# Token-major residual stream and output projections in a three-layer hybrid kernel

## The chip, the cores and the metric

One core of a Trainium2 chip. The metric is the device time of one launch, in microseconds (us), as the median of the runs shown. TensorE (PE in the profile), VectorE (DVE), ScalarE (ACT) and GpSimd (POOL) compute; SP issues most of the loads.

## What is computed

A sequence of 512 tokens of width 2048 passes through three layers, in float32. The first mixes attention (16 heads) with a gated recurrence (8 heads), the other two mix retention (6 heads), differential attention (4 heads) and a linear recurrence with a convolution. All have the same frame, and the first has a gated addition behind it:

```python
u = rmsnorm(h, g_pre);  z = u @ w_in          # z is split into q, k, v, gates, ...
y = concat(mixers(z)) @ w_out
h = h + rmsnorm(y, g_post)
# first layer only
gate = sigmoid(h @ w_pg);  e = p_l @ w_pp
h = h + rmsnorm(gate * e, g_ple)
```

The norms are over the 2048 channels of a token.

## The kernel before

Every large product is made of three: each float32 operand is split into a rounded part and a rest (`whi`, `wlo` for weights, `uh`, `ul` for activations), and `uh*whi + ul*whi + uh*wlo` is summed in PSUM. `wpiece` (line 212) loads a piece of weights of 512 KB on SP and splits it, ACT making `whi` (line 238) and DVE `wlo` (line 239). There are two raw buffers; while `self.extra` is set (the output stages of the first layer and of layer 0 of the second block) every third piece uses a set of its own.

TensorE's order is written by hand; the other engines are ordered by a scheduler by priority. Two products exist. `proj` (line 243) keeps weights as the stationary operand and gives channels by tokens, 128 x 512, in 16 steps over the input channels. `projT` (line 303) keeps activations stationary and gives tokens by channels; it is used for values, 256 columns at a time (`hg_round` line 580, `att_round` line 449, `qkv` line 1187), and for the last output projection.

The mixers run in the shadow of projections: they are generators in a queue (`add`, `unit`, `tick`, lines 111 to 129). Each projection step credits its time with `tick`, and when the credit exceeds `self.spacing` (2.9, 3.25 or 4.6 us by stage) one unit of mixing is emitted between matmuls. `gates` (line 731) forces units until the head that it needs is done.

Up to the last layer the residual stream `X` is channel-major (16 tiles of 128 channels by 512 tokens), as is `U`, its split. An output stage is `rows` (line 778): one `proj` of four tiles, five of two, then `proj_halves` (line 278) for the last two tiles, in two token halves. ACT squares every tile, POOL sums the squares (line 793), and `col_rstd` (line 766) sums them over channels with a matmul of ones (line 772) and takes Ln and Exp. `carry` (line 837) then has POOL scale each tile by the row factor (line 821), DVE add it to the stream (line 822), and ACT and DVE split the sum (`split`, lines 830 to 835), first for tokens 0 to 255, then for the rest. The next projection starts with twelve of its 16 steps on the first token half (`half_first`, `NH = 12`) and does their second half at its end. `spill` (line 859) stores the stream and squares it for the next norm; `stream_stats` (line 872) finishes that norm at step 12 of the recurrence's second projection (`lru`, line 1069).

The last output stage is `last_rows` (line 1388) and already token-major: `projT` for 1792 columns, the stream turned back by 64 transposes (line 1408), then the last 256 columns by token group (lines 1433 to 1435), where each group of 128 tokens ends with its sum, its factor (a power on POOL, line 1441) and its residual adds (line 1446).

The input stage is `load_x` (line 334): x comes token-major, TensorE turns it by 64 transposes (line 362), ACT and DVE split it, and it is stored channel-major for later.

## Time and profile before

| | us |
|---|---|
| median of 3 runs | 3137.11 (3136.86 to 3137.35) |
| the profiled execution | 3136.49 |
| its span, first to last instruction | 3134.7 |
| TensorE busy | 3053.4 (97%) |
| DVE / ACT / POOL busy | 1907.1 / 1521.9 / 808.4 |
| mean granted TensorE clock | 0.991 |

A profiled execution is a run of its own, so its time stands beside its span. Matmuls are pipelined: their durations overlap, and the distance between two starts is what one costs. Idle time of an engine matters only where the engine sets the end.

### The profile page before, as it was taken

How to read it: one execution, taken by the hardware profiler on the slowest of the kernel's cores; microseconds unless marked ns; L12 is line 12 of the kernel's file. 1: busy time of each engine (PE TensorE's matmuls, PEld its weight loads, DVE VectorE, ACT ScalarE, POOL GpSimd, SP SyncE). 2: the span in 40 equal slices, each digit the busy share in tenths (PEclk: the TensorE clock that was granted, in tenths of full speed). 3: DMA queues.
4: the chain of work that ended last, by engine and by line, in shares of the span. 5: the costliest groups of instructions: out<-in, count | busy, mean ns of one | idle time of the engine just before them, and what ended most of it. 6: DMA issues, size and time to landing. Idle time of an engine off the chain costs nothing. (4 is left out here: it accounts for less than half of the span.)

```text
span 3134.7 us, 45170 instructions
## 1 busy us (share of the span) xinstructions
PE 3053.4 (97%) x17004; PEld 2660.5 (85%) x17004; DVE 1907.1 (61%) x3321; ACT 1521.9 (49%) x2731; POOL 808.4 (26%) x838
## 2 busy tenths in 40 slices
PE   8999999999999999998899999999989999999998
PEld 7888888888888888887688888878877888888898
DVE  5778788577776327458775456542478654565434
ACT  5354343455556335446555434653465545346532
POOL 1555456110110204127430011011264200111101
PEclk9999999999999999999999999999999999999999
DMA  6222222332332533335342233243353322332433
GB/s 209 77 72 74 75 75 72 104 96 85 85 90 75 170 99 118 123 104 163 95 118 85 84 108 95 81 149 108 108 177 90 108 88 81 108 95 81 131 112 115
DMA packets 296776, 327.67 MB, mean 105 GB/s; under 512 B 17823, under 2 KB 277998, under 8 KB 296430
## 3 DMA queue, kind: packets, MB, share of 16 engines
q1 hardware_dynamic: 277518, 275.74, 28.4%
q0 software_dynamic: 16864, 45.37, 5.0%
q10 hardware_dynamic: 2176, 3.68, 0.4%
q8 instruction: 133, 2.18, 0.3%
q14 instruction: 85, 0.70, 0.1%
HBM read 292.23 MB, written 16.78 MB: 99 GB/s over the span
## 5 line engine op out<-in xcount | busy, mean ns | idle before, releaser
L239 DVE TENSOR_TENSOR wlo<-raw,whi 128x512 fp32r<-128x512 f32 x1028 | 806.5, 792 | 790.5 <-ACT whi L238 772.4
L270 PE MATMUL acc<-ul,whi 128*128 128x512 f32 (+1 forms) x3056 | 1167.6, 382 | 27.9 <-DVE ul L835 21.6
L269 PE MATMUL acc<-uh,whi 128*128 128x512 f32 (+1 forms) x3056 | 1183.3, 387 | 9.2 <-ACT whi L238 7.5
L271 PE MATMUL acc<-uh,wlo 128*128 128x512 f32 (+1 forms) x3056 | 1168.3, 382 | 14.1 <-DVE wlo L239 13.8
L238 ACT ACTIVATE whi<-raw 128x512 fp32r<-128x512 f32 x1028 | 635.8, 627 | 985.0 <-PE acc L270 570.1
L270 PEld LDWEIGHTS acc<-ul,whi 128*128 128x128 f32 x3056 | 580.5, 190 | 133.7 <-DVE ul L835 23.3
L271 PEld LDWEIGHTS acc<-uh,wlo 128*128 128x128 f32 x3056 | 579.2, 190 | 132.4 <-DVE wlo L239 20.7
L269 PEld LDWEIGHTS acc<-uh,whi 128*128 128x128 f32 x3056 | 580.0, 190 | 114.4 <-ACT whi L238 9.2
L318 PE MATMUL acct<-whi,uh 128*128 128x256 f32 (+1 forms) x1536 | 446.2, 290 | 1.7 <-DVE gt L738 1.1
L319 PE MATMUL acct<-wlo,uh 128*128 128x256 f32 (+1 forms) x1536 | 442.1, 288 | 1.6 <-DVE wlo L239 1.6
L320 PE MATMUL acct<-whi,ul 128*128 128x256 f32 (+1 forms) x1536 | 442.1, 288 | 0.0
L318 PEld LDWEIGHTS acct<-whi,uh 128*128 128x128 f32 x1536 | 294.8, 192 | 5.9 <-DVE gt L738 1.5
L319 PEld LDWEIGHTS acct<-wlo,uh 128*128 128x128 f32 x1536 | 294.9, 192 | 5.5 <-DVE wlo L239 1.8
L320 PEld LDWEIGHTS acct<-whi,ul 128*128 128x128 f32 x1536 | 294.7, 192 | 2.6
L742 POOL TENSOR_TENSOR mx<-mx,gt 128x512 f32<-128x512 f32 x48 | 65.3, 1362 | 599.1 <-ACT gt L739 591.9
L793 POOL TENSOR_TENSOR ssq<-ssq,sq 128x512 f32<-128x512 f32 x39 | 52.4, 1343 | 383.4 <-ACT sq L976 254.4
L821 POOL TENSOR_TENSOR mx<-mx,rbo 128x256 f32<-128x256 f32 x96 | 90.9, 984 | 80.5 <-ACT rbo L209 80.5
L635 POOL TENSOR_TENSOR w<-w,t 128x512 f32<-128x512 f32 x56 | 69.4, 1239 | 70.1 <-DVE zz L627 69.9
L1168 POOL TENSOR_TENSOR q<-q,rt 128x512 f32<-128x512 f32 x20 | 31.6, 1581 | 214.5 <-DVE rt L1167 208.9
L636 POOL TENSOR_TENSOR w<-w,t 128x512 f32<-128x512 f32 x56 | 78.5, 1402 | 19.6 <-DVE zz L628 19.6
L462 POOL TENSOR_TENSOR zsw<-zsw,ropes 80x512 f32<-80x512 f32 x16 | 28.1, 1757 | 214.0 <-DMA zsw<-q 115.8
L1168 POOL TENSOR_TENSOR k<-k,rt 128x512 f32<-128x512 f32 x20 | 31.6, 1579 | 140.9 <-DVE rt L1167 100.9
(388 smaller groups left out, 3906.9 us busy)
## 6 DMA issues: line engine op xcount, KB each, us to landing
raw<-in_w_in SPq DMA_DIRECT2D x304, 512.0 KB
raw<-in_w_out SPq DMA_DIRECT2D x88, 512.0 KB
raw<-in_w_in SPq DMA_DIRECT2D x120, 256.0 KB
raw<-in_w_pg SPq DMA_DIRECT2D x28, 512.0 KB
raw<-in_w_out SPq DMA_DIRECT2D x32, 256.0 KB
x<-x_stream POOLq DMA_DIRECT2D x32, 256.0 KB, 6.9
x_stream<-x POOLq DMA_DIRECT2D x32, 256.0 KB, 5.6
raw<-in_w_pg SPq DMA_DIRECT2D x28, 256.0 KB
```

The source lines that it names most:

```text
L238: nc.scalar.activation(hi, r, AF.Copy)
L239: nc.vector.tensor_tensor(lo, r, hi.bitcast(F32), op=ALU.subtract)
L269: nc.tensor.matmul(d, wk[k][0][:, s], uh, start=st, stop=False, skip_group_check=half_first)
L270: nc.tensor.matmul(d, wk[k][0][:, s], ul, start=False, stop=False, skip_group_check=half_first)
L271: nc.tensor.matmul(d, wk[k][1][:, s], uh, start=False, stop=sp, skip_group_check=half_first)
L318: nc.tensor.matmul(dst[t], uh[:, s], wk[k][0], start=st, stop=False, skip_group_check=True)
L319: nc.tensor.matmul(dst[t], uh[:, s], wk[k][1], start=False, stop=False, skip_group_check=True)
L320: nc.tensor.matmul(dst[t], ul[:, s], wk[k][0], start=False, stop=sp, skip_group_check=True)
L635: G.tensor_tensor(hv2(w2, m, 1), hv2(w2, m, 1), ev.to_broadcast([P, nb, m]), op=ALU.mult)
L636: G.tensor_tensor(hv2(w1, m, 0), hv2(w1, m, 0), od.to_broadcast([P, nb, m]), op=ALU.mult)
L742: nc.gpsimd.tensor_tensor(self.mixed[k], self.mixed[k], t, op=ALU.mult)
L821: nc.gpsimd.tensor_tensor(y, y, rb[:, s], op=ALU.mult)
```

## The change

- `X` becomes token-major (four tiles of 128 tokens by 2048 channels) in all layers. `tok_rows` replaces `rows` and `last_rows`: three `projT` of 512 columns, one of 256, then the last 256 columns by token group with weights held in buffers of their own. Each group ends with its factor and four residual adds on DVE. `proj_halves`, `col_rstd`, `carry`, `residual`, `spill` and the extra weight buffers go.
- New rows are transposed by TensorE in pairs of token groups and split straight from PSUM into `U` (`new_rows`): tokens 0 to 255 while the last two token groups run (`first_half`), the others inside the next stage. At the gate projection they stand between steps of the p projection (`ple_cols`, now token-major too); at the recurrence projection between its steps (`lru_entry`, with `NH = 4`).
- `keep_stream` stores the stream and takes its squares with ACT's accumulator; `token_stats` makes the row factors with POOL's power and turns them to a row by four small matmuls.
- Values are projected 512 columns at a time where two rounds can share it (`head_v`): twice in the first layer's recurrence, once each in retention and differential attention, per layer. The attention of the first layer keeps 256.
- The input comes channel-major from memory, as do p and the parameter columns, so the input needs no transpose and is not stored. The first weight piece is loaded step by step, between tiles of x, on one queue. Ten matmuls of ones run before the first product. The squares of x are summed by DVE during the second projection.
- The spacings become 3.2 (from 3.25) and 4.4 (from 4.6); 2.9 stays.

```diff
+        with tc.high_priority(offset=3 * BIG):
+
+            nc.scalar.activation(self.cp.tile([P, 1], F32, name="act0"), self.ones[:, 0:1], AF.Copy)
+            ps = self.bank()
+            for i in range(WARM):
+                nc.tensor.matmul(ps[:, (i % 4) * P:(i % 4) * P + P], self.ones, self.ones, start=True, stop=True)
...
+            raw = self.wp.tile([P, nk, n], F32, tag="raw", name="raw", bufs=2)
+            start = self.pieces == 1
+            for r in ([slice(i, i + 1) for i in range(nk)] if start else [slice(0, nk)]):
+                for j, c in enumerate(cols):
+                    src = wap[(k0 + r.start) * P:(k0 + r.stop) * P, c:c + cw].rearrange("(a p) c -> p a c", p=P)
+                    self.in_order(start, lambda: nc.sync.dma_start(raw[:, r, j * cw:(j + 1) * cw], src))
+                if start:
+                    self.more_input()
...
-    def projT(self, wap, c0, U, cb, kts=range(KT), cw=256):
+    def projT(self, wap, c0, U, cb, kts=range(KT), cw=512, before=None):
...
-            for k in range(nk):
+            steps = [(k, t) for k in range(nk) for t in range(4)]
+            if n == 1 and i in (0, KT - nk):
+                steps = [(k, t) for t in range(4) for k in range(nk)]
+            for j, (k, t) in enumerate(steps):
+                if before and j % 4 == 0:
+                    before(i + j // 4)
                 uh, ul = U[kts[i + k]]
+                s = slice(t * P, (t + 1) * P)
+                st, sp = i + k == 0 and t % n == 0, i + k == KT - 1
+                nc.tensor.matmul(dst[t], uh[:, s], wk[k][0], start=st, stop=False, skip_group_check=True)
+                nc.tensor.matmul(dst[t], uh[:, s], wk[k][1], start=False, stop=False, skip_group_check=True)
+                nc.tensor.matmul(dst[t], ul[:, s], wk[k][0], start=False, stop=sp, skip_group_check=True)
+                if sp and n == 1:
+                    with self.hp():
+                        cb(t, dst[t])
+                if j % 4 == 3:
+                    self.tick(1.3 * cw / 256)
+        if n > 1:
+            with self.hp():
                 for t in range(4):
-                    s = slice(t * P, (t + 1) * P)
-                    st, sp = i + k == 0 and t % n == 0, i + k == KT - 1
-                    nc.tensor.matmul(dst[t], uh[:, s], wk[k][0], start=st, stop=False, skip_group_check=True)
-                    nc.tensor.matmul(dst[t], uh[:, s], wk[k][1], start=False, stop=False, skip_group_check=True)
-                    nc.tensor.matmul(dst[t], ul[:, s], wk[k][0], start=False, stop=sp, skip_group_check=True)
-                self.tick(1.3 * cw / 256)
-        with self.hp():
-            for t in range(4):
-                cb(t, dst[t])
+                    cb(t, dst[t])
...
+        def load():
+            tag, nb, n = homes.pop(0)
+            k = len(xt)
+            t = xp.tile([P, n, T], F32, tag=tag, name="xt", bufs=nb)
+            src = A["kc_xt"][:, k:k + n, :]
+            for i in range(n):
+                xt[k + i] = t[:, i]
+            if k < 5:
+                with self.tc.high_priority(offset=(2 if k else 3) * BIG):
+                    self.in_order(True, lambda: nc.sync.dma_start(t, src))
             else:
-                nc.gpsimd.dma_start(xt, x[:, :, c:c + n])
-            xts.append(xt)
+                with self.tc.issue_after(self.row_done.ins):
+                    S_.dma_start(t, src)
+
+        self.more_input = load
...
         def row(k):
...
-            i = max(j for j in range(nch) if chunks[j][0] <= k * P)
-            o = k * P - chunks[i][0]
-            ps = self.bank()
-            for t in range(4):
-                nc.tensor.transpose(ps[:, t * P:(t + 1) * P], xts[i][:, t, o:o + P], self.ident)
+            if k not in xt:
+                load()
...
+        def square(k):
+
+            with self.tc.issue_after(self.whis[-1].ins):
+                S_.activation(ssq if k == 0 else xt[k], xt[k], AF.Square)
+            if k:
+                with self.tc.issue_after(self.wlos[-1].ins):
+                    V.tensor_tensor(ssq, ssq, xt[k], op=ALU.add)
...
-        self.proj(w, [OFF1["hq"] + 256 * r, OFF1["hff"] + 256 * r], U, both, before=before)
+        self.proj(w, [OFF1["hq"] + 256 * r, OFF1["hff"] + 256 * r], U, both, before=before, first=first)
         self.proj(w, [OFF1["hfb"] + 256 * r], U, fcb(fbs, 8), before=stats)
-        vt = pool.tile([P, 4, 256], F32, tag="vh", name="vh", bufs=2)
+        if r % 2 == 0:
+            self.head_v(pool, "vh", w, OFF1["hv"] + 256 * r, U, 2 * r, 4)
+        for m in range(2):
+            self.add(self.hg_head(pool, 2 * r + m, qs[m], fs[m], fbs[m], self.vts.pop(2 * r + m)))
...
+    def head_v(self, pool, tag, wap, c0, U, h0, n, bufs=6):
...
+            for h in range(n):
+                self.nc.scalar.activation(vts[h][:, t, :], ps[:, h * P:(h + 1) * P], AF.Copy, scale=self.rc[:, t:t + 1])
+
+        self.projT(wap, c0, U, vcb, cw=n * P)
...
+    def load_tokens(self, pool, src):
+        X = [pool.tile([P, D], F32, name=f"x{t}") for t in range(4)]
+        for t in range(4):
+            self.nc.gpsimd.dma_start(X[t], src[t * P:(t + 1) * P, :])
+        return X
+
+    def tok_rows(self, pool, wap, gi, U, order, evac, X, fresh, before=None, more=None, at=None):
...
+        gains(0)
+        for c in (0, 512, 1024):
+            gains(c + 512)
+            if more:
+                more(c)
+            self.projT(wap, c, U, lambda t, acc, c=c: out(t, c, 512, acc), range(KT) if c else order,
+                       before=None if c else before)
+        if more:
+            more(1536)
+        self.projT(wap, 1536, U, lambda t, acc: out(t, 1536, 256, acc), cw=256)
+        self.drain()
+        wl = []
+        for i in range(0, KT, 4):
+            wl.extend(self.wpiece(wap, i, 4, [1792], 256, (pool, i)))
+        for t in range(4):
+            acc = self.accp.tile([P, T], F32, tag="acc", name="accl")[:, 0:256]
+            for i in range(KT):
+                if at:
+                    at(t, i)
+                hi, lo = wl[i]
+                uh, ul = (u[:, t * P:(t + 1) * P] for u in U[i])
+                nc.tensor.matmul(acc, uh, hi, start=i == 0, stop=False)
+                nc.tensor.matmul(acc, uh, lo, start=False, stop=False)
+                nc.tensor.matmul(acc, ul, hi, start=False, stop=i == KT - 1)
+            with self.tc.high_priority(offset=2 * BIG):
+                out(t, 1792, 256, acc)
+                r = pool.tile([P, 2], F32, tag="r", name="r", bufs=2)
+                self.tok_rstd(r[:, 1:2], r[:, 0:1], ss[:, t, :])
+                for i in ((0, 1, 2, 3) if t < 2 else (1, 2, 3, 0)):
+                    x = X[t][:, i * T:(i + 1) * T]
+                    V.scalar_tensor_tensor(x, yt[t][i], r[:, 1:2], x, op0=ALU.mult, op1=ALU.add)
+                    fresh(t, i)
+
...
+    def new_rows(self, U, X, pair, g, k):
+
+        nc = self.nc
+        s = HALF[pair]
...
             ps = self.bank()
...
+            for i in range(2):
+                for t in range(2):
+                    nc.tensor.transpose(ps[:, (2 * i + t) * P:(2 * i + t + 1) * P],
+                                        X[2 * pair + t][:, (k + i) * P:(k + i + 1) * P], self.ident)
+            for i in range(2):
+                uh, ul = (u[:, s] for u in U[k + i])
+                src = ps[:, i * 256:(i + 1) * 256]
+                if g is None:
+                    nc.scalar.activation(uh, src, AF.Copy)
+                    nc.vector.tensor_tensor(ul, src, uh.bitcast(F32), op=ALU.subtract)
+                else:
+                    gc = g[:, k + i:k + i + 1]
+                    nc.scalar.activation(uh, src, AF.Copy, scale=gc)
+                    nc.vector.scalar_tensor_tensor(ul, src, gc, uh.bitcast(F32), op0=ALU.mult, op1=ALU.subtract)
+
+    def first_half(self, U, X, g):
+
+        def at(t, i):
+            n = 16 * (t - 2) + i - 9
+            if n >= 0 and n % 2 == 0 and n < 16:
+                self.new_rows(U, X, 0, g, n)
+        return at
+
+    def keep_stream(self, pool, X):
+
+        self.ss = self.cp.tile([P, 4, 4], F32, name="ssx")
+        for t in range(4):
+            for i in range(4):
+                sq = pool.tile([P, T], F32, tag="sq", name="sq")
+                self.nc.scalar.activation(sq, X[t][:, i * T:(i + 1) * T], AF.Square, accum_out=self.ss[:, t, i:i + 1])
+            self.nc.gpsimd.dma_start(self.xs_dram[t * P:(t + 1) * P, :], X[t])
...
+    def token_stats(self):
...
+        for t in range(4):
+            c = slice(t * P, (t + 1) * P)
+            nc.vector.tensor_scalar(rb[:, c], self.ident, self.rc[:, t:t + 1], None, op0=ALU.mult)
+            nc.tensor.matmul(ps[:, c], self.ones, rb[:, c], start=True, stop=True)
+        nc.scalar.activation(rb, ps, AF.Copy)
+
+    def lru_entry(self, l, U, X):
+
+        g = self.col["pre_norm_g_2"][:, 16 * l:16 * l + 16]
+        ks = list(range(NH, KT, 2)) + list(range(0, NH, 2))
 
         def before(i):
...
+            if i >= 2 and ks:
+                self.new_rows(U, X, 1, g, ks.pop(0))
+
+        self.lru_first(l, U, lambda run: run(before=before, half_first=True))
...
-            U, then = self.carry(*res, X)
-            res = self.rows(pool, A["w_pg"][0], U, range(KT), gated, then, late)
-            U, then = self.carry(*res, X, self.col["pre_norm_g_2"][:, 0:16])
-            self.lru_first(0, U, then)
-            self.extra = None
+
+            self.tok_rows(pool, A["w_out"][0], 0, U, order, self.plain(sq), X, lambda t, i: None, more=load,
+                          at=self.first_half(U, X, None))
+            ks = list(range(0, KT, 2))
+            n = 0
+            for c in (0, 1):
+                for _ in self.ple_cols(pool, c, es):
+                    n += 1
+                    if n >= 3:
+                        self.new_rows(U, X, 1, None, ks.pop(0))
+
+            def before(i):
+                if ks:
+                    self.new_rows(U, X, 1, None, ks.pop(0))
+
+            def more(c):
+                self.drain()
+                if c in (512, 1024):
+                    self.spacing = 6.0
+                    self.add(self.ple_cols(pool, c // 512 + 1, es))
+
+            self.tok_rows(pool, A["w_pg"][0], 1, U, range(KT), gated, X, lambda t, i: None, before, more,
+                          self.first_half(U, X, self.col["pre_norm_g_2"][:, 0:16]))
+            self.lru_entry(0, U, X)
+            self.keep_stream(pool, X)
         return U
...
-        self.projT(w, v, U, vcb)
-        return rot, vt
+        if nv:
+            self.head_v(pool, "v", w, v, U, h0, nv, vbufs)
+        return rot
...
-                    self.spacing = 3.25
...
+                    self.spacing = 3.2
...
+                self.spacing = 4.4
                 for r in range(2):
...
-            self.extra = pool if l == 0 else None
             U = self.u_tiles()
...
+            at = None if l else self.first_half(U, X, self.col["pre_norm_g_2"][:, 16:32])
+            self.tok_rows(pool, A["w_out_2"][l], 2 + l, U, order, self.plain(sq), X, store if l else lambda t, i: None,
+                          at=at)
             if l == 0:
-                X = self.load_stream(pool)
-                res = self.rows(pool, w, U, order, self.plain(g), lambda run: run())
-                U, then = self.carry(*res, X, self.col["pre_norm_g_2"][:, 16:32])
-                self.lru_first(1, U, then)
-            else:
-                self.last_rows(pool, l, w, U, order)
-            self.extra = None
+                self.lru_entry(1, U, X)
+                self.keep_stream(pool, X)
         return U
...
-NH = 12
+NH = 4
```

## Rows read from the trace of the kernel before

**Rows 1.** Page, part 1: span; busy time, share and instructions by engine.

```profile
PE 3053.4 (97%) x17004; PEld 2660.5 (85%) x17004; DVE 1907.1 (61%) x3321; ACT 1521.9 (49%) x2731; POOL 808.4 (26%) x838
```

**Rows 2.** Waits of TensorE, whole span: us in total, times, longest.

```profile
PE acc L270 <- DVE ul L835: 21.6, 7, 7.3
PE acc L271 <- DVE wlo L239: 13.8, 9, 5.0
PE acc L269 <- ACT whi L238: 7.5, 4, 3.1
PE acc L270 <- DVE ul L831: 6.3, 4, 2.0
```

**Rows 3.** Windows: stretch, length, busy us (count) of PE, PEld, DVE, ACT, POOL; clock, DMA share, GB/s.

```profile
1207.00:1237.00 30.00, 23.68 (x154) 21.82 (x153) 29.36 (x48) 18.23 (x39) 18.88 (x20) 0.89 0.39 123
1408.00:1444.00 36.00, 21.85 (x151) 19.96 (x150) 35.37 (x56) 24.88 (x47) 22.95 (x25) 0.90 0.36 112
...
2268.00:2300.00 32.00, 21.57 (x143) 20.20 (x142) 32.00 (x48) 21.44 (x42) 21.31 (x24) 0.85 0.37 115
...
1502.00:1544.00 42.00, 31.49 (x125) 24.23 (x125) 39.49 (x58) 19.00 (x30) 21.91 (x17) 0.88 0.24 70
...
2355.00:2400.00 45.00, 39.89 (x169) 30.31 (x168) 44.40 (x65) 19.28 (x32) 20.63 (x18) 1.00 0.30 88
2933.00:3101.00 168.00, 165.94 (x1213) 157.08 (x1212) 54.98 (x88) 61.74 (x172) 11.71 (x18) 1.00 0.39 123
```

**Rows 4.** Timeline of TensorE: start, duration; 512 columns, then 256 columns.

```profile
58.24 0.39 PE L271 MATMUL acc<-uh,wlo 128*128 128x512 f32 x1
...
60.51 0.39 PE L269 MATMUL acc<-uh,whi 128*128 128x512 f32 x1
...
450.14 0.28 PE L320 MATMUL acct<-whi,ul 128*128 128x256 f32 x1
...
451.94 0.28 PE L320 MATMUL acct<-whi,ul 128*128 128x256 f32 x1
```

**Rows 5.** Timeline of TensorE, input stage: one group of transposes and what follows.

```profile
15.17 0.60 PE L362 MATMUL mb<-kc_ident,xt 128*128 128x128 f32 x4
15.53 0.48 PE L269 MATMUL acc<-uh,whi 128*128 128x512 f32 x1
15.85 0.39 PE L270 MATMUL acc<-ul,whi 128*128 128x512 f32 x1
```

**Rows 6.** Timeline of TensorE, gate entry: column sums and the next product.

```profile
1218.94 0.59 PE L772 MATMUL mb<-ssq,ones 128*128 128x256 f32 x2
...
1220.05 0.47 PE L269 MATMUL acc<-uh,whi 128*128 128x256 f32 x1
```

**Rows 7.** Timeline, start of the kernel, ACT and TensorE.

```profile
9.06 1.15 ACT L238 ACTIVATE whi<-raw 128x512 fp32r<-128x512 f32 x2 [1.38 <-DMA raw<-in_w_in]
...
11.39 0.78 PE L269 MATMUL acc<-uh,whi 128*128 128x512 f32 x1
...
13.78 0.40 PE L269 MATMUL acc<-uh,whi 128*128 128x512 f32 x1
```

**Rows 8.** Timeline of DVE, gate entry: the same weight split beside POOL and without.

```profile
1211.36 1.22 DVE L239 TENSOR_TENSOR wlo<-raw,whi 128x512 fp32r<-128x512 f32 x1
...
1214.90 0.68 DVE L239 TENSOR_TENSOR wlo<-raw,whi 128x512 fp32r<-128x512 f32 x1
```

**Rows 9.** Timeline, last projection: row sum of a token group, its residual adds.

```profile
3113.50 0.19 ACT L1415 ACTIVATION_READ_ACCUMULATOR sq<-accl 128x1 f32 x1
...
3115.07 3.11 DVE L1446 SCALAR_TENSOR_TENSOR xt<-mx,r,xt 128x512 f32<-128x512 f32 x3 [0.67 <-POOL r L1441]
```

**Rows 10.** Timeline of TensorE, end of one head of the first block.

```profile
490.58 1.06 PE L660 MATMUL mb<-zz 128*128 128x128 f32 x8
...
494.23 1.05 PE L667 MATMUL mb<-zz 128*128 128x128 f32 x8
...
516.01 0.39 PE L721 MATMUL mb<-sqs,ones_r 128*128 128x512 f32 x1
```

More of the change, by code (lines that the diff above doesn't have):

```diff
@@ L258, in proj @@
             mk = [(m, k) for k in range(nk) for m in range(nm)]
-            if i == 0 and not half_first or i + nk == len(steps):
+            if i == 0 and not half_first and not first or i + nk == len(steps):
                 mk = [(m, k) for m in range(nm) for k in range(nk)]
@@ L398, in stack_q @@
+        return row
     def stack_q(self, pool, z):
@@ L562, in stats @@
         def stats(i):
-            if first and i == 10:
+            if first and i in (0, 4, 8):
+                for k in range(6 * (i // 4), min(6 * (i // 4) + 6, KT)):
+                    self.input_square(k)
+            if first and i == 12:
                 self.input_stats()
@@ L835, in split @@
             nc.vector.scalar_tensor_tensor(ul, src, gc, uh.bitcast(F32), op0=ALU.mult, op1=ALU.subtract)
-    def carry(self, ys, rb, second, X, pre=None):
-        U = self.u_tiles()
-        def half(ks, s):
-            for k in ks:
-                self.residual(ys, rb, X, k, s)
-                self.split(U, k, X[k], s, pre)
-        half(range(KT), HALF[0])
-        def then(run):
-            def before(i):
-                if i == 5:
-                    second()
-                    half(list(range(NH, KT)) + list(range(NH)), HALF[1])
-                    if pre is not None:
-                        self.spill(X)
-            run(before=before, half_first=True)
-        return U, then
-    def spill(self, X):
-        nc = self.nc
-        ssq = self.cp.tile([P, T], F32, name="rb")
-        for k in range(KT):
-            nc.gpsimd.dma_start(self.xs_dram[:, k, :], X[k])
-            if k == 0:
-                nc.scalar.activation(ssq, X[k], AF.Square)
-            else:
-                nc.scalar.activation(X[k], X[k], AF.Square)
-                nc.gpsimd.tensor_tensor(ssq, ssq, X[k], op=ALU.add)
-        self.rb = ssq
     def stream_stats(self):
@@ L966, in first_block @@
[L966 to L977 removed]
+            es = {}
@@ L1012, in ple_rows @@
-            es.append(e)
-        return es
+                uh, ul = (u[:, s] for u in self.pT[k])
+                nc.tensor.matmul(ps, uh, wk[k][0], start=k == 0, stop=False)
+                nc.tensor.matmul(ps, uh, wk[k][1], start=False, stop=False)
+                nc.tensor.matmul(ps, ul, wk[k][0], start=False, stop=k == 1)
+            es[t, c] = pool.tile([P, T], F32, tag="e", name="e", bufs=EB)
+            nc.scalar.activation(es[t, c], ps, AF.Copy)
+            yield
     def log_sigmoid8(self, pool):
```

436 lines of the change are left out of this document (139 added, 297 removed).

## Prediction

> **What bounds the kernel now.** I read the page's table of busy time first: TensorE is busy 97% of the span, no other engine over 61% [rows 1]. So a change pays only by taking instructions off TensorE or by closing one of its gaps, 81 us in all (3134.7 - 3053.4). The table of waits says who ends the gaps [rows 2]: the splits of new activation rows (lines 831 and 835, 27.9 us together) and the splits of weights (lines 238 and 239, 21.3 us). The windows say where [rows 3]. The first three are the entries into the gate projection and into the recurrence projection of layers 0 and 1, where the last row sums, the norm, the residual and the new splits stand between two projections: TensorE idles 6.3, 14.2 and 10.4 us there (length minus busy), 30.9 together, and the granted clock falls to 0.89, 0.90 and 0.85. The next two are the recurrence stretches of the two layers, 10.5 and 5.1 us idle. The last is the final output projection, already token-major: 2.1 us idle in 168.
>
> Busy time is no measure of a matmul here, since matmuls overlap. The pace is read from start times [rows 4]: ten 512-column products take 60.51 - 58.24 = 2.27 us, 0.227 each; fifteen 256-column ones 451.94 - 450.14 = 1.80, 0.120 each. Two narrow ones cost 0.240 against 0.227 for the wide one that does their work.
>
> The profiled execution took 3136.49 us, 0.6 under the median of 3137.11. I sum against it and give the result from the median.
>
> **TensorE's own instructions.**
> - Wide values. Six pairs of 256-column value projections (two in the first block, two in each layer) become one 512-column projection each: 384 x 0.120 = 46.1 us against 192 x 0.227 = 43.6, so 2.5 a pair, **-15.0**. The Trainium skill ("TensorE: Matmul & The Clock Gate", section "Back-to-back issue gap") states N/2.4 ns plus 2.5 for spaced matmuls, which is 109 and 216 ns as an estimate. By it a pair would save 0.5 us, six pairs 3.0, and my sum would be 12 smaller. The trace's 120 and 227 ns differ from it, and the measurement decides.
> - Output projections. In the new form each stage has 576 wide and 384 narrow products: 130.8 + 46.1 = 176.9. Before, the two plain stages had 672 and 192 (175.6), the gate stage 528 and 480 (177.5), the last one 192 and 1152 (181.8): +1.3, +1.3, -0.6, -4.9. Splitting only 4 of 16 steps by token halves at each recurrence entry saves 96 wide against 192 narrow, 1.2, twice. Together **-5.3**.
> - Transposes. A group of four costs 15.85 - 15.17 - 0.227 = 0.45 us with the slowed matmul behind it [rows 5]. Out go 13 groups of the input stage behind the first product, 16 of the last stage and 2 of p; in come 48 (three stages, two token pairs, eight column pairs): 17 x 0.45 = **+7.6**.
> - Column sums. The ones matmuls of line 772 take 1220.05 - 1218.94 = 1.11 us, six times [rows 6]: **-6.7**. The other statistics matmuls only change places; I count nothing, bounds 2 either way.
>
> Together -19.4.
>
> **Start.** The first product starts at 11.39 us, after weights that are split at 9.06 [rows 7]. The new stage asks for 256 KB of x and 256 KB of weights first, not the 512 KB piece, needs no transpose, and warms TensorE with ten matmuls of ones. Bounds: nothing, if latency is all of it, and 9.1, if only the 2.3 us from split to product stay. By bytes, 512 instead of 768 KB ahead of the first split, 9.06 shrinks by 3.0; three groups of transposes less are 1.4, half a piece to split instead of a whole 0.5: 4.9. Between 11.39 and 13.78 six products take 2.39 us instead of 1.36, 1.0 more, which the warming should give back. One stall of 0.6 behind weights goes with the smaller pieces. **-6.5**. The x loads move to SP and ACT and the stores of x vanish; what is queued behind them on SP is weights, in the order of use.
>
> **Entries.** Before, the last two columns of a stage need row sums by TensorE, Ln and Exp, then POOL multiplies per tile; while POOL runs, DVE's weight split takes 1.22 us, otherwise 0.68 [rows 8]. Now the last 256 columns run by token group; two groups' rows are done while the other two run. From [rows 9], the path from a group's accumulated square to its first residual add is 3115.07 - 3113.50 = 1.6 us, about 2.1 from the last product; 3.11/3 = 1.04 an add beside POOL, and below it without. Each token group runs 48 x 0.120 = 5.8 us, so the first pair is hidden. For the second pair, the recurrence entry has two half steps, 2 x 12 x 0.120 = 2.9 us, as cover before a transpose that needs the first add (2.1 + 1.0 = 3.1): I keep 3 us there, twice (the gated evacuation adds one ACT and two DVE operations). The gate entry has two p-projection steps, 2 x 6 x 0.227 = 2.7 us, yet its first transpose reads columns 0 to 255, whose add is last in the order (1, 2, 3, 0): 2.1 + 4 x 0.68 (the split without POOL, as bound) to 1.04 = 4.8 to 6.3, a wait of 2.1 to 3.6; with ACT's copies and splits queued behind, 4.5. Of 30.9 idle I so keep 10.5. The lost clock is bounded by 0 and by 0.11 x 30 + 0.10 x 36 + 0.15 x 32 = 11.7; part of that lies in the idle time itself, so I take 8. **-28.4**.
>
> **Recurrence stretches** [rows 3]: of 15.6 idle I take 7 away. The row scales now come from POOL's power and one transposing broadcast, without Ln and Exp and without 16 POOL adds, but the layer's convolution, angle tables and gate weights still crowd DVE. Bounds 0 and 15.6. **-7**.
>
> **What gets worse.** (a) First block: mixing work is issued in units, one per 2.9 us of credited projection time. A head has 14 units, eight heads 112. Credit behind the first heads was 3 x 83 + 83 = 332 us, enough for 114; removing two projections of 20.8 and doubling one leaves 311, 107 units. So the last gate must force the final half dozen units with no matmul beside them. In [rows 10] that chain runs from 490.58 to 516.01, 25.4 us, of which TensorE works some 8: bounds 0 and 17. Steps are 494.23 - 490.58 = 3.65 apart because they wait for a tick, not for data, so I take 7. (b) A wide value projection needs all four banks, the last two just used by k; its rotary evacuations on DVE must clear them within 5.5 us: 0 to 4, I take 2. (c) The input's sum of squares now needs 16 ACT and 16 DVE operations inside one 22 us projection: 0 to 4, I take 1.5. (d) The tail has four adds on DVE where POOL took one; without POOL beside them they are shorter: 0. **+10.5**.
>
> Sum: -19.4 - 6.5 - 28.4 - 7 + 10.5 = -50.8. From the median: 3137.1 - 50.8 = **3086**.
>
> **Rivals.**
> - *The entries don't close.* The second pair's chain (add, transpose, split) is as late as today's. For: it is still serial over four engines, with a first transpose that wants the last add. Against: half the rows are finished earlier, and POOL's per-tile multiplies leave. Then 28.4 stays: 3115. Chance 0.15.
> - *DVE was the brake throughout.* With POOL's row work gone, DVE's 0.68 holds everywhere, and both the 10.5 and the other 8.6 us go too: 3067. For: 1.22 against 0.68. Against: POOL keeps its convolution moves and gate multiplies. The Trainium skill ("SBUF — State Buffer", section "SBUF: two separate sides") calls the port pair of DVE and POOL an exclusive lock; the pair of durations agrees. Chance 0.15.
> - *The wide values give nothing*, because the banks are waited for at each of the six: 15 stay, 3101. Against: 4 to 5.5 us for two evacuations. Chance 0.10.
> - *Slower: weights starve.* Three stages lose their third set of weight buffers, 32 pieces each, 96. A piece must land and be split in the 5.5 us of its matmuls; 50.8/96 = 0.53 us late per piece is the point where the gain is gone; at 0.8 late it is 3137 - 51 + 77 = 3163. Against: the last stage has lived on two sets and idles 2.1 us in 168 [rows 3]; its pieces have the same bytes. Chance 0.07.
>
> **How the numbers follow.** The forecast has 0.53: its unknowns (start 0 to 9.1, entries, 7 of the drain between 0 and 17, 7 of 15.6) give about 18 either way, 3068 to 3104. The range takes in the faster rival and most of the late entries above: **3060 to 3116**, leaving out the starving weights and the ends of the others. A measurement can tell 0.2%, 6.3 us. Faster takes all but the slower rival and a tail of the late entries: 0.90. Same 0.04, slower 0.06.
>
> **What would show it.** Right: TensorE's first product before 8 us; pace unchanged; transposes in groups of four at 0.45; the three entry windows with under 5 us idle each; line 239 at 0.68 in them; a new gap of some 7 us where the first block's last gate ends. Wrong: gaps spread through the output projections behind weight loads (starving), gaps at the six wide projections behind DVE or ACT (banks), entry gaps of the old size ended by the residual add, or a drain above 15 us.

## The result, and the profile after

The changed kernel takes 3082.42 us (median of 4 runs, 3080.56 to 3089.22) against 3137.23 for the kernel before on the same chip: ratio 0.9827, 95% interval 0.9814 to 0.9839, so 54.8 us less. The forecast was 3086. The profiled execution took 3081.94 us, with a span of 3080.2 against 3134.7; the difference of the two spans, 54.5, is what is followed below.

The page's busy time, where [rows 1] stood:

```profile
PE 3022.6 (98%) x15454; PEld 2571.7 (83%) x15454; DVE 1831.7 (59%) x3277; ACT 1437.5 (47%) x2629; POOL 578.0 (19%) x603
```

TensorE has 1550 instructions less and POOL over a quarter less work. The waits of TensorE, against [rows 2]:

```profile
engine line waited for: us in total, times, longest us
PE do L1354 <- DVE mx L730: 8.6, 2, 4.5
PE acct L309 <- ACT whi L250: 6.7, 2, 3.7
PE acc L283 <- DVE wlo L251: 6.4, 11, 1.4
PE mb L841 <- DVE x L823: 4.1, 3, 1.9
...
PE mb L680 <- DVE zz L630: 3.8, 1, 3.8
PE acct L309 <- DVE rt L1194: 2.9, 4, 1.0
PE acct L309 <- DVE hf L531: 2.5, 1, 2.5
```

The 27.9 us behind the splits of new rows are gone from the top of the list. In their place stand waits that the kernel before did not have at this size: a head's norm in differential attention (L730), the first weights of an output projection (L250 before L309), the first block's last units (L630). The windows that answer to [rows 3] are the three entries, the two recurrence stretches and the last output projection:

```profile
core 0: us, PE busy (x) PEld busy (x) DVE busy (x) ACT busy (x) POOL busy (x), PEclk, DMA share, GB/s
1187.00:1203.00 16.00, 13.81 (x73) 10.78 (x72) 9.45 (x21) 10.16 (x24) 0.00 (x0) 1.00 0.18 50
1366.00:1400.00 34.00, 30.51 (x264) 29.91 (x263) 28.18 (x63) 20.16 (x58) 3.97 (x7) 1.00 0.43 154
2211.00:2240.00 29.00, 26.60 (x232) 26.23 (x231) 21.49 (x48) 13.27 (x38) 3.42 (x6) 1.00 0.45 164
1405.00:1524.00 119.00, 113.54 (x521) 92.66 (x520) 75.15 (x119) 55.63 (x100) 28.37 (x26) 0.99 0.39 108
2250.00:2362.00 112.00, 109.81 (x514) 90.15 (x513) 73.86 (x115) 53.89 (x98) 28.37 (x27) 1.00 0.40 114
2890.00:3071.00 181.00, 177.78 (x962) 154.22 (x960) 67.24 (x106) 56.39 (x110) 5.90 (x9) 0.99 0.38 129
```

The entries idle 2.2, 3.5 and 2.4 us, 8.1 together where 30.9 stood, and the clock in them is 1.00. The start:

```profile
1.04 4.28 PE L113 MATMUL mb<-ones 128*128 128x128 f32 x20 [1.04 <-DVE mhalf L118]
6.63 0.50 PE L281 MATMUL acc<-uh,whi 128*128 128x512 f32 x1 [1.31 <-ACT whi L250]
```

The first product starts at 6.63 us instead of 11.39 [rows 7].

To see where the 54.5 us come from, TensorE's time is split in two. Each instruction is given the usual distance to the next start for its line and width (the median of all its kind in the same trace): that sum is **own time**. What a distance has beyond it is **lost time**: gaps and slowed matmuls. Counted from the first product:

| us | before | after | difference |
|---|---|---|---|
| first product | 11.39 | 6.63 | -4.8 |
| own time | 3012.1 | 2985.9 | -26.2 |
| lost: start and first round | 6.8 | 4.1 | -2.7 |
| lost: rest of the first block's recurrence | 2.5 | 10.3 | +7.8 |
| lost: attention, first output and gate projections | 4.6 | 1.2 | -3.4 |
| lost: the three entries | 41.4 | 10.7 | -30.7 |
| lost: the two recurrence stretches | 25.8 | 13.2 | -12.6 |
| lost: retention and differential attention | 11.8 | 28.1 | +16.3 |
| lost: the layers' output projections | 7.6 | 11.0 | +3.4 |
| behind the last matmul | 10.3 | 9.0 | -1.3 |

The differences add up to 54.2; the rest is rounding. Own time is 25.1 less in weight products and 7.8 in column sums, 7.3 more in transposes (68 more, 17 groups). The pace is what it was: 0.227 us for 512 columns, 0.120 for 256 (0.113 to 0.117 in the last columns, taken by token group). A group of transposes with the slowed product behind it:

```profile
1178.66 0.28 PE L816 MATMUL accl<-whi,ul 128*128 128x256 f32 x1
1178.78 0.60 PE L841 MATMUL mb<-kc_ident,x 128*128 128x128 f32 x4
1179.14 0.37 PE L814 MATMUL accl<-whi,uh 128*128 128x256 f32 x1
1179.34 0.28 PE L815 MATMUL accl<-wlo,uh 128*128 128x256 f32 x1
```

1179.34 - 1178.78 = 0.56, less 0.117 for the product: 0.44 us a group.

The first row of the table is the least certain one: in the traces of the experiments that leave the first 100 us alone, the first product starts between 5.43 and 7.05 us and the first 100 us lose 3.7 to 6.8, 10.8 to 13.3 together; the changed kernel's own 10.7 lies at the low end.

### The profile page after: what moved, and what is told of

Its sections match the earlier page's. It is cut to its first block, busy times and chain, and to the rows that moved or that the text cites. A ratio compares the mean times of both kernels' runs of the same rounds, so it can differ in the third digit from the quotient of the medians.

```text
span 3080.2 us, 41214 instructions
## 1 busy us (share of the span) xinstructions
PE 3022.6 (98%) x15454; PEld 2571.7 (83%) x15454; DVE 1831.7 (59%) x3277; ACT 1437.5 (47%) x2629; POOL 578.0 (19%) x603
## 4 chain that ended last, share of the span: by engine, by line
PE 87%; DVE 5%; ACT 3%; DMA 3%; issue 1%; POOL 0%; SPq 0%; DVEq 0%; POOLq 0%; ACTq 0%
PE acc L283 15%; PE acc L281 15%; PE acc L282 15%; PE acct L309 10%; PE acct L310 10%; PE acct L311 10%; PE mb L662 2%; DVE wlo L251 1%; PE mb L488 1%; DMA raw<-in_w_out 1%; PE accl L814 1%; PE accl L815 1%; PE accl L816 1%; DVE rt L1194 1%; PE mb L841 1%
## 5 line engine op out<-in xcount | busy, mean ns | idle before, releaser
L250 ACT ACTIVATE whi<-raw 128x512 fp32r<-128x512 f32 x976 | 602.5, 628 | 1122.9 <-PE acc L282 439.3
L281 PE MATMUL acc<-uh,whi 128*128 128x512 f32 (+1 forms) x2272 | 899.5, 396 | 5.2 <-ACT whi L250 4.0
L283 PE MATMUL acc<-uh,wlo 128*128 128x512 f32 (+1 forms) x2272 | 885.0, 390 | 6.4 <-DVE wlo L251 6.4
L282 PE MATMUL acc<-ul,whi 128*128 128x512 f32 (+1 forms) x2272 | 881.8, 388 | 0.0
L309 PE MATMUL acct<-whi,uh 128*128 128x512 f32 (+1 forms) x1792 | 634.6, 354 | 12.1 <-ACT whi L250 6.7
L310 PE MATMUL acct<-wlo,uh 128*128 128x512 f32 (+1 forms) x1792 | 631.8, 353 | 1.9 <-DVE wlo L251 1.9
L311 PE MATMUL acct<-whi,ul 128*128 128x512 f32 (+1 forms) x1792 | 631.3, 352 | 0.0
L283 PEld LDWEIGHTS acc<-uh,wlo 128*128 128x128 f32 x2272 | 428.6, 189 | 101.7 <-DVE wlo L251 11.8
L281 PEld LDWEIGHTS acc<-uh,whi 128*128 128x128 f32 x2272 | 429.5, 189 | 87.0 <-ACT whi L250 5.0
L282 PEld LDWEIGHTS acc<-ul,whi 128*128 128x128 f32 x2272 | 429.8, 189 | 80.3 <-issue 0.2
L309 PEld LDWEIGHTS acct<-whi,uh 128*128 128x128 f32 x1792 | 339.9, 190 | 60.4 <-ACT whi L250 7.6
L814 PE MATMUL accl<-whi,uh 128*128 128x256 f32 x256 | 73.1, 285 | 0.0
```

Of the source, the lines that this page charges most:

```text
L250: self.whis.append(nc.scalar.activation(hi, r, AF.Copy))
L281: nc.tensor.matmul(d, wk[k][0][:, s], uh, start=st, stop=False, skip_group_check=half_first)
L282: nc.tensor.matmul(d, wk[k][0][:, s], ul, start=False, stop=False, skip_group_check=half_first)
L283: nc.tensor.matmul(d, wk[k][1][:, s], uh, start=False, stop=sp, skip_group_check=half_first)
L309: nc.tensor.matmul(dst[t], uh[:, s], wk[k][0], start=st, stop=False, skip_group_check=True)
L310: nc.tensor.matmul(dst[t], uh[:, s], wk[k][1], start=False, stop=False, skip_group_check=True)
```

## The experiments

All edits are made to the changed kernel. Each run was timed beside runs of the kernel before, on chips that differ by a few us, so "longer" and "shorter" are differences of the ratio to 0.9827, times 3137 us. An interval of a ratio is about 0.0013 either way, 4 us, and a difference of two ratios is uncertain by nearly 6; where less than that matters, the trace decides. In the windows of e1, e7 and e8 lost time adds up only what is above the usual distance; in the table and elsewhere, what is below it is taken off.

**e1: the drain of the first block.**

```diff
-            self.spacing = 2.9
+            self.spacing = 2.5
```

> One unit of mixing per 2.5 us of credit in the first block's recurrence instead of 2.9, nothing else. Theory (the last gate forces some six units with no matmul beside them): by counting credits none is forced any more, the 4.1 us gap at 549 us of the profile and the slow stretch behind it go, and the time falls by 5 to 8 us against the changed kernel. Rival (a unit's chain over DVE, ACT and POOL is what is slow, 3.65 us a step in the trace of before): the units run into each other between the matmuls, gaps of 0.5 us and more appear from 150 to 450 us, and the time is the same or up to 5 us longer.

Ratio 0.9848 (0.9832 to 0.9863): 6.6 us **longer**, a little beyond the uncertainty. The end's gap went, as the theory says (lost time from 500 to 600 us falls from 9.2 to 2.8), and the rival's gaps came: lost time from 200 to 500 us rises from 7.2 to 19.3. TensorE's waits from 120 to 600 us in this run:

```profile
PE mb L724 <- DVE sqs L719: 5.3, 4, 2.2
PE ho L701 <- ACT as L691: 2.1, 2, 1.9
PE acc L281 <- DVE hf L531: 0.8, 1, 0.8
```

In the changed kernel the same stretch has one wait of 3.8 us (L680 behind zz) and two small ones, all at the end. So the drain is what it was said to be, and closer units are no cure: a head's norm, split on DVE, isn't ready 2.5 us later.

**e2: narrow values at the same places.**

```diff
-        self.projT(wap, c0, U, vcb, cw=n * P)
+        for a in range(0, n, 2):
...
+            self.projT(wap, c0 + a * P, U, vcb, cw=256)
```

> The six wide value projections are made as two of 256 columns each, one behind the other, at the same places. Theory (two narrow products cost 0.240 us, the wide one 0.227): TensorE's own time grows by 15.0 us; the gaps of 1.3 to 2.8 us ahead of the wide projections, which wait for all four banks, some 9 us in all, shrink, so that the time grows by 6 to 15. Rival 1 (the bank waits eat what the wide form saves): within 2 us of the changed kernel. Rival 2 (the gap rule of the Trainium skill, 2.5 ns a matmul): own time grows by 3.0 only, and the time does not grow.

Ratio 0.9862 (0.9845 to 0.9878): 11.0 longer. Own time from the first product is 3000.4, 14.5 more; lost time falls by 1.7 only. The 15.0 of the forecast is confirmed in size, and both rivals fall. The Trainium skill ("TensorE: Matmul & The Clock Gate", section "Back-to-back issue gap") gives N/2.4 ns plus 2.5 for the gap of an isolated matmul; an estimate by it is 3.0, and this trace does not agree with it.

**e3: transposes twice.**

```diff
-            for i in range(2):
+            for i in (0, 1, 0, 1):
```

> Each group of four transposes of new rows is done twice into the same bank (48 groups more). Theory (transposes lie on TensorE's path at 0.36 to 0.45 us a group): 17 to 22 us longer. Rival (the half of them that stands in the entries is hidden in waits that TensorE has there anyway): 8 to 11 us longer.

Ratio 0.9865 (0.985 to 0.988): 11.9 longer. Own time rises by 21.3, 48 x 0.444, so the price of a group is right; lost time falls by 9.8, since the entries' gaps at 1187 to 1199 and 2232 us shrink or close (one at 1441 us closes too, as it does in other runs). The truth lies between theory and rival, nearer to the rival: TensorE had waits in the entries that took in part of the groups.

**e4: all rows late.**

```diff
-                          at=self.first_half(U, X, None))
+                          at=None)
+            for k in range(0, KT, 2):
+                self.new_rows(U, X, 0, None, k)
```

and the same at the other two stages.

> The rows of tokens 0 to 255 are transposed and split after the last token group's matmuls at all three entries, not beside them; the number of instructions is the same. Theory (the entries closed because half of the rows is done early): eight groups of two splits each stand in each entry, on DVE 0.8 us a group or more, so 4 to 8 us of idle time a stage, 12 to 24 us in all. Rival (the entries closed because POOL's per-tile multiplies left and DVE splits faster): 0 to 4 us longer.

Ratio 0.9878 (0.9863 to 0.9892): 16.0 longer. The three entries in this run:

```profile
1184.00:1214.00 30.00, 23.77 (x116) 19.06 (x115) 17.29 (x41) 16.87 (x44) 0.55 (x1) 0.89 0.13 41
1366.00:1410.00 44.00, 38.82 (x316) 37.40 (x315) 29.37 (x64) 22.85 (x66) 4.55 (x8) 0.93 0.50 180
2211.00:2256.00 45.00, 37.66 (x305) 36.71 (x305) 27.08 (x55) 22.28 (x66) 4.57 (x8) 0.90 0.49 176
```

Idle 6.2, 5.2 and 7.3 us, 18.7 instead of 8.1, and the clock is back at 0.89 to 0.93, close to what it was before the change [rows 3]. POOL has as little to do here as in the changed kernel. In lost time the entries come to 28.7, against 41.4 in the kernel before and 10.7 in the changed one. So having half the rows early closed 18 of the 31 us. The other 13 are gone with all rows late too, and no run tells which part of the change took them.

**e7 and e9: POOL's load.** Four useless multiplies of 128x192 with each group of new rows; in e7 on a tile of their own, in e9 reading the rows that are to be transposed.

```diff
+            for t in (0, 1, 0, 1):
+                x = X[2 * pair + t][:, k * P:k * P + 192]
+                nc.gpsimd.tensor_tensor(self.scr, x, x, op=ALU.mult)
```

> POOL makes four useless multiplies of 128x192 on a tile of its own with each group of new rows (192 in all), as busy as it was with the residual multiplies of the kernel before. Rival (the entries closed because POOL's work left them and DVE is no longer slowed): the weight split beside them goes from 0.68 towards 1.2 us, the entries open again by 3 us or more each, 9 to 20 us in all. Theory (they closed because half the rows is done early and the rest stands between steps): DVE slows as much, but the entries open by under 1.5 us each, 0 to 5 us in all.

Ratio 0.9857 (0.9843 to 0.987): 9.4 longer, but not for the reason asked about: nothing held the multiplies, and all 192 ran between 3.7 and 206 us. Lost time up to 300 us is 18.9 against 8.8 (7.8 to 11.8 in the other runs that keep the first block's spacing); the entries are as they were. It tells that POOL's work in the first rounds is dear, nothing else.

> As the run before with POOL's useless multiplies, which had run in the first 206 us because nothing held them back; now each reads the rows that are about to be transposed (128x192 of one token group), so that it can't run before their residual add. Rival (the entries closed because POOL's work left them): weight splits and row splits on DVE slow from 0.68 towards 1.2 us in the entries and each of the three opens by 3 us or more, 9 to 20 us in all. Theory (half the rows early, the rest between steps): DVE slows as much, the entries open by under 1.5 us each, 0 to 5 us in all.

Ratio 0.9826 (0.9813 to 0.984): no difference, -0.3. Here the multiplies lie in the three entries (first and last start in the row). The second row is the residual add in the changed kernel, the third the same add in this run, the last two the weight split in the first and in the third of this run's entries:

```profile
L841 POOL TENSOR_TENSOR scr<-x x192: 495/507/992, 1169.0 to 2276.1; 128x192 f32<-128x192 f32 x192
```
```profile
L823 DVE SCALAR_TENSOR_TENSOR x<-mx,r,x x64: 743/746/753, 1166.0 to 3075.2; 128x512 f32<-128x512 f32 x64
```
```profile
L824 DVE SCALAR_TENSOR_TENSOR x<-mx,r,x x64: 739/801/1000, 1168.2 to 3078.0; 128x512 f32<-128x512 f32 x64
...
L252 DVE TENSOR_TENSOR wlo<-raw,whi x23: 675/693/909, 1149.7 to 1227.6; 128x512 fp32r<-128x512 f32 x23
...
L252 DVE TENSOR_TENSOR wlo<-raw,whi x7: 675/818/1189, 2247.1 to 2259.5; 128x512 fp32r<-128x512 f32 x7
```

Columns are minimum, median and maximum in ns. The adds beside POOL take up to 1.00 us instead of 0.75. The splits mostly stay near 0.69 in the first entry, and in the third one reaches 1.19. "DVE slows as much" was too much: the median stays far from 1.22, so the run does not repeat the old load in full. In its trace the entries lose some 6 us more than in the changed kernel, most of it in the second one, but in e10 and e12, whose entries are the changed kernel's, they lose 4.7 more as well. So this load doesn't bring the old entries back; what the full old load on DVE would do there was not tested.

**e5, e6, e10: differential attention.** In the changed kernel TensorE waits 4.1 us at 1932 (4.5 at 2769). PE, ACT and DVE there:

```profile
1927.13 0.40 PE L724 MATMUL mb<-sqs,ones_r 128*128 128x512 f32 x1
...
1930.44 0.63 ACT L250 ACTIVATE whi<-raw 128x512 fp32r<-128x512 f32 x1 [1.76 <-DMA raw<-in_w_in]
1931.09 1.28 ACT L220 ACT_TABLE_LOAD   x1
1932.39 0.69 ACT L220 ACTIVATE sq<-mb,kc_cols 128x512 f32<-128x512 f32 x1
1933.09 1.28 ACT L221 ACT_TABLE_LOAD   x1
1934.39 0.63 ACT L221 ACTIVATE sq<-sq 128x512 f32<-128x512 f32 x1
...
1935.05 0.75 DVE L730 SCALAR_TENSOR_TENSOR mx<-do,gs,sq 128x512 f32<-128x512 f32 x1 [2.85 <-ACT sq L221]
...
1935.95 0.46 PE L1354 MATMUL do<-pT,v 128*128 128x128 f32 x2 [4.05 <-DVE mx L730]
```

The sums are ready at 1927.5. The logarithm and the exponential that make the norm's factor (Ln, L220, and Exp, L221) run on ACT. The Ln stands in ACT's queue behind a weight split that waits for its load until 1930.44; Ln and Exp each load a table, and the next head's matmul wants the bank that `mx` frees.

```diff
-                self.spacing = 4.4
+                self.spacing = 4.6
```

> Differential attention's spacing goes back from 4.4 to 4.6 us. The changed kernel has two new gaps of 4.3 and 4.8 us (at 1932 and 2769 us), where the first head's norm is late for the next head's bank; slowed matmuls follow, 13.6 us for both against 4.6 for the four gaps of the kernel before. Theory (what matters is how long after the evacuations of the second k projection that norm falls: 13 units of 4.4 put it 8 us behind, 13 of 4.6 put it 10.5 behind, as before): both gaps shrink under 2 us and the time falls by 5 to 9 us; the last gate may force two units, 1 to 2 us. Rival (the gaps come from the missing second value projection, which used to stand there): they stay over 4 us each and the time moves by less than 3 us.

Ratio 0.9814 (0.98 to 0.9827): 4.1 shorter, inside the uncertainty, so the trace decides. TensorE's waits from 1800 to 2100 us:

```profile
PE mb L723 <- ACT sqs L718: 3.3, 1, 3.3
PE do L1354 <- DVE mx L730: 1.7, 2, 1.2
```

The wait of 4.1 is now two of 1.7 together, and the distance to k's evacuations has moved as planned: DVE's part of the norm (L719) starts 7.1 us behind the last evacuation of k (L1191), as in the kernel before; in the changed kernel it is 3.5. (The 10.5 and 8 of the expectation are counted from credits.) So that distance is the cause. But two units are forced by the last gate, and with no matmul beside them they lose 5.2 us a layer.

```diff
-                       0, 0 if r else 4, 4)
+                       2 * r, 2, 4)
```

(and the columns of `dv` with `256 * r`)

> In differential attention alone, values are projected in each round again, 256 columns at a time, with the spacing of 4.4. Rival of the run above (the missing value projection is the cause): the two gaps go, 9 us, the bank waits of 1.4 us ahead of the wide projections go, twice, own time grows by 2 x 2.5: 5 to 8 us shorter. Theory (the distance to k's evacuations is the cause, and it stays 8 us): the gaps stay, and the time is 0 to 5 us longer.

Ratio 0.9806 (0.9793 to 0.9819): 6.6 shorter, what the rival gave, but not by its mechanism: the wait on `mx` stays (3.7 us at 1912), as the theory says, and the distance from k is 3.5 us as in the changed kernel. What went is the late start of the output projection, 5.7 and 5.4 us of lost time at 2073 and 2912, which neither had reckoned with.

> Differential attention wholly as in the kernel before: values in each round, 256 columns, and the spacing of 4.6. Each alone took one of two gaps: 4.6 the late norm (some 9 us for both layers), the values in each round the late start of the output projection behind units forced at the end (10 us for both). Theory: both go, against 5.2 us of own time: 12 to 17 us shorter than the changed kernel. Rival (one gap takes the place of the other): 7 to 9 us shorter, as with the values in each round alone.

Ratio 0.9775 (0.9762 to 0.9789): 16.3 shorter (12.5 by the spans of the two profiles). With both edits the waits from 1800 to 2100 us are

```profile
PE do L1354 <- DVE mx L730: 1.7, 2, 1.2
PE acct L310 <- DVE wlo L251: 0.2, 1, 0.2
```

Lost time over the whole run is 61.7 against 78.4, own time 5.6 more. The output projection's late start, on the chain that ended last of the changed kernel, and POOL's queue there:

```profile
2061.97 13.97 DMA raw<-in_w_out
```
```profile
2059.72 1.67 POOL L744 TENSOR_TENSOR mx<-mx,gt 128x512 f32<-128x512 f32 x1 [8.50 <-DVE mx L730]
2061.34 2.18 POOL L771 DMA_DIRECT2D x<-x_stream  x4
```

A weight piece is on its way for 13.97 us beside four loads of 1 MB of the stream, which POOL can issue only behind the last gate's multiply, and that waits for the last head's norm. In e10 the loads go out 7.0 us earlier, at 2054.36, the piece takes 11.69 us and nobody waits long. Other weight pieces on that chain take 3.3 to 4.2 us (6.85 at the kernel's start), so the slow one beside the stream's loads is shown; that the loads' issue time alone decides is argued, since no run moved it alone.

**e8: crowding at the gates alone.**

```diff
+            self.spacing = 2.4
             self.gates(pool, w, OFF1["hg"], 8, 8, U)
```

> The spacing of the first block's recurrence stays 2.9 and falls to 2.4 at its gates alone, where no evacuation of f stands in DVE's and ACT's queues. By counting credits one unit is forced at the end instead of seven. With 2.5 everywhere the end's gap went and new gaps of 0.5 to 2.6 us came at 215 to 515 us. Theory (units can be crowded where DVE is freer): the end's gap falls from some 7 to 2 us and under 2 us come instead, 3 to 6 us shorter than the changed kernel. Rival (a unit's own chain is too long for 2.4 us anywhere): gaps between 450 and 550 us take up what the end gains, within 2 us.

Ratio 0.9818 (0.9804 to 0.9831): 2.8 shorter, inside the interval. In the trace lost time falls from 9.2 to 2.0 between 500 and 600 us and rises from 2.3 to 5.2 between 400 and 500: 4.3 gained. The theory holds in that stretch, a little weaker than put; over the whole run the trace's lost time is 78.0 against 78.4, since other stretches vary by as much.

**e11: together.** e10, e8, and in `tok_rows`

```diff
-                for i in ((0, 1, 2, 3) if t < 2 else (1, 2, 3, 0)):
+                for i in ((0, 1, 2, 3) if t < 2 or gi == 0 else (1, 2, 3, 0)):
```

> Differential attention as before, the spacing 2.4 at the first block's gates, and the residual adds of all token groups of the first output projection in the order of the columns, since its next stage reads column 0 first. Theory: the gains add up: 12 to 17 from differential attention, about 2 from the gates, 1 to 2 at the gate entry: 15 to 20 us shorter than the changed kernel. Rival: no more than differential attention alone gives.

3063.39 us (3062.4 to 3064.93), ratio 0.9761 (0.9748 to 0.9775): 20.7 shorter than the changed kernel. Of its three waits of 0.6 to 0.7 us at the gate entry two are left, of 0.8. Lost time is 55.6 against 61.7 in e10. The times of e11 and e10 differ by 4.4, inside the uncertainty, so they don't refute the rival.

**e12: no warming.**

```diff
-WARM = 10
+WARM = 0
```

> The ten matmuls of ones ahead of the first product are left out (WARM = 0). Theory (the engine's clock is low at the start, and it is the matmuls of ones that pay for it): the first six products take some 2.4 us instead of 1.4, as in the kernel before, and the time grows by 1 us, less than can be told from the times; the first product starts no earlier. Rival (the warming does nothing): the same pace of 0.227 us from the first product on.

Ratio 0.9825 (0.9811 to 0.9838): not to be told from the changed kernel. Two starts of this run, six products apart, and a window over the first twelve:

```profile
8.78 0.63 PE L281 MATMUL acc<-uh,whi 128*128 128x512 f32 x1
...
11.34 0.55 PE L281 MATMUL acc<-uh,whi 128*128 128x512 f32 x1
```
```profile
6.00:11.30 5.30, 5.25 (x12) 4.09 (x13) 2.88 (x5) 2.69 (x4) 0.00 (x0) 1.00 1.04 347
```

The first distance is 0.59 us, the next eleven 0.43, then comes full pace. From the first product to the thirteenth it takes 5.29 us, in the changed kernel 3.13: 2.2 more. The first product of this run starts 0.6 earlier, at 6.05, which is inside the scatter of the runs, so the thirteenth is 1.6 late. Of that 1.0 is left behind the first value projection's wait, at 82.55 instead of 81.55, where the runs with warming and the same code up to there lie between 81.2 and 81.8, but for e4 at 84.0.

## Why the prediction was right

The number was right, and so was most of the mechanism; inside the sum errors cancel: some 22 us more were gained than forecast, and some 18 lost that were not foreseen.

- *TensorE's own* -19.4: measured -26.2. Wide values and output projections were put at -20.3, the products fell by 25.1; e2 confirms 14.5 of the 15.0 for the values. The narrow products that are left cost 0.118 on the mean (340.4 us for 2879) against 0.120 before (725.0 for 6047), which the sum did not have. Transposes +7.6 (7.3) and column sums -6.7 (-7.8) held.
- *Start* -6.5: -4.8 at the first product and -2.7 of lost time in the first round, with the four-bank wait of the first wide value projection already in it, and with (c), which no run separates. The warming was put at 1.0; e12 gives 2.2, of which about 1.0 lasts. As traces of the same start differ by up to 2.6 us, the agreement of this term is in part luck.
- *Entries* -28.4: -30.7. For 18 of it e4 gives the reason that the text gave: half the rows earlier. The other 13 have no run of their own. The 10.5 us of idle time kept there were 8.1. The rival that the entries don't close falls, and so does the one that DVE was the brake throughout, since its time of 3067 was not reached and 8.1 us stay.
- *Recurrence stretches* -7 of 15.6 idle: 7.7 are left, so -8.0, and -12.6 of lost time with the clock, which the term left out. In windows of the same length POOL's busy time falls from 67.8 and 62.7 us to 28.4 each, DVE's from 88.9 and 85.0 to 75.2 and 73.9; no run tells which of it matters.
- *(a) The drain* +7: +7.8, and the new gap stands where it was announced. TensorE waits 3.84 us for `zz`, then for the norm:

```profile
553.39 2.81 PE L680 MATMUL mb<-zz 128*128 128x256 f32 x8 [3.84 <-DVE zz L630]
...
561.32 0.50 PE L723 MATMUL mb<-sqs,ones_r 128*128 128x512 f32 x1 [1.35 <-ACT sqs L718]
```

- *(b) Four banks* +2: this is the step that failed. Lost time in retention and differential attention rose by 16.3. The banks are part of it: lost time just ahead of and inside the wide projections of retention and differential attention is 1.8 and 1.3 us a layer. The larger part is a thing the forecast didn't ask about: it counted the units of mixing for the first block alone. The spacing of 4.4 instead of 4.6 moves the first head's norm from 7.1 to 3.5 us behind k's evacuations, where its Ln stands behind a late weight split: 13.6 us of lost time in both layers against 4.6. That it is the spacing, and not the value projection taken out of the second round, e5 and e6 show. The missing projection does something else (e6): the last head's norm comes late, and with it the stream's loads, so the layers' output projections, put at nothing, lose 5.7 and 5.3 us at their start, 3.4 more than they lost in all before.
- *Wide values give nothing*, *weights starve*: e2 rules out the first; for the second, lost time in the first two output stages fell, and gaps behind weight splits in them are missing, so the third buffers were not needed. No run with other buffers was tried.

The 6.3 us that can be told apart were passed almost nine times over.

## What to carry to other kernels

When one projection is merged or removed, or the spacing of the work behind it is changed, the work that rode in its shadow moves too: write down for every stage, not only the longest, at which moment each of its chains now ends and what stands in the in-order queues at that moment. A merged product can be worth its full price on the engine while the place where it stood was worth more: in differential attention the merging and the new spacing took 5.6 us off TensorE's own time, and undoing both made the kernel 16.3 us faster. And a row of new data that is needed in pieces should be turned and split in pieces while the last products run: half of it early was worth 16 us here.

## What was not expected of the hardware

- Without warming TensorE ran its first twelve products 0.43 us apart (0.59 behind the first), the pace of its lower level (1.2 GHz; 0.227 is that of 2.4), while the granted clock of that window reads 1.00: the column does not show the slow start, only the distances of starts do. After 4.28 us of small matmuls of ones and 1.31 us of waiting, the changed kernel was at 0.23 from the fourth product on.
- A gap of 4.1 us behind busy matmuls cost more than itself. In the changed kernel's window right behind it the clock is 0.72, with products 0.43 us apart:

```profile
1936.00:1942.00 6.00, 6.00 (x21) 4.81 (x22) 1.75 (x3) 0.68 (x2) 0.00 (x0) 0.72 0.28 91
```

  The entries' gaps of up to 2.38 us left it at 1.00.
- DVE's adds of two operands from SBUF slowed beside POOL from 0.746 to as much as 1.000 us in e9, the row splits, which read one operand from PSUM, not at all (0.42 to 0.48 in both runs). In the kernel before, the row splits read both operands from SBUF, and beside POOL they took up to 0.96 us instead of 0.41. The first row is from that kernel, the second from e9, where POOL works beside all of them:

```profile
L831 DVE TENSOR_TENSOR ul<-x,uh x32: 410/414/964, 1202.9 to 1250.8; 128x256 fp32r<-128x256 f32 x32
```
```profile
L852 DVE TENSOR_TENSOR ul<-mb,uh x32: 409/421/425, 1176.0 to 1209.1; 128x256 fp32r<-128x256 f32 x32
```

  Split straight from PSUM, the rows no longer slow beside POOL. The Trainium skill ("SBUF — State Buffer", section "SBUF: two separate sides") limits the lock to DVE operations with two SBUF inputs or in a two-port mode; these rows agree.
